# Reordering the scan step of a hybrid decoder kernel: where the held work, the spread and the meta rows stand

## The chip, the core and the metric

The kernel runs on one core of one Trainium2 chip. The metric is the device time of one execution in microseconds (us); the time given for a kernel is the median of its runs. A core has five engines that work through their own queues in order: TensorE (PE in the profile, with its weight loads shown apart as PEld), VectorE (DVE), ScalarE (ACT), GpSimd (POOL) and SyncE (SP, which here only issues DMAs).

## The reference

One decoder layer over 16 learned meta tokens and 512 tokens of width 1024, in float32. The part that matters here is the Mamba-2 branch: a projection, a causal convolution of four taps with SiLU, and a state-space scan in chunks of 128 positions, with the 16 meta tokens as a short chunk in front.

```python
u = rmsnorm(h, mix_norm_w)
proj = u @ w_in                      # pool | z | xbc | dt | gates
gates = sigmoid(proj[..., OFF_GATE:] + b_gate)
...
xbc = silu(causal_depthwise_conv(xbc, conv_w, conv_b))   # x (2048), B (8 x 128), C (8 x 128)
dt = softplus(dt_raw + dt_bias); a = -exp(a_log)
# per chunk, group g (8 of them) and head r (4 per group):
a_cs = cumsum(dt * a)
y_diag = einsum(C B^T, exp(a_cs_l - a_cs_s) masked, x * dt)
states = einsum(B, exp(a_cs_last - a_cs), x * dt)
# states are carried from chunk to chunk: prev = decay * prev + states
y_off = einsum(C, prev, exp(a_cs))
y = (y_diag + y_off + x * d_skip) * silu(z)
y = rmsnorm_per_group(y) * norm_w
...
h = h + (gate_pool * y_pool + gate_ssd * (y @ w_ssd_out)) @ w_o
h = h + square(relu(rmsnorm(h) @ w_ff1)) @ w_ff2
out = rmsnorm(h)[:, 16:]
```

## The kernel before

Every large product is made of three matmuls on parts: each float32 operand is split in a high part (a cast on ACT) and a low part (a subtraction on DVE), and high x high, low x high and high x low are summed in PSUM. Weights come in blocks of 128 x 1024 (`raw`, three buffers); `block()` hands out the next prepared block, and, with `depth` 2, first issues the DMA, the ACT cast `whi` (L75) and the DVE subtraction `wlo` (L76) of the block two places further on.

The work is staged: the first projections (group 0's tiles and three gates) on unnormalised input, then a loop over the eight SSD groups `g` (L640), then the pooling branch, the output projection, and the MLP. The change lies in the loop. In iteration `g` the kernel does the scan of group `g` and, in between, the projections of group `g+1`, so that PE has matmuls while ACT and DVE prepare the scan. The order on PE, ACT and DVE is the order of the program (`manual_schedule`); on each of these engines an instruction that waits holds up everything behind it.

The parts of one iteration, by the names of the code and the profile:

- `turn` (L416): PE turns B's three chunks and its meta rows (`ptb`), x's meta rows (`ptm`) and x's four chunks (`ptx`); ACT copies the meta rows to `bm` and the chunks to `btok`; DVE scales x's meta rows (`xdm`, then three parts `xm`), x's chunks by dt (`xdt`), by the decay (`xdd`), and forms the low part of `bm`.
- `steps`: the four projections for group `g+1`, in the order B (`bt`), C (`ct`), and the two tiles of x (`xc`), all called `px` on PE (L157 to L160; 48 matmuls each). Each returns its convolution: one ACT instruction (L347) and three on DVE (L350), all four of which read the projection's PSUM tile. In iteration 4 the steps are eight parts of the first half of the output projection (`pso`), and in iteration 7 eight parts of the second (`psp`); the first step of iteration 7 (`two`) does two parts.
- `spread` (L452): two exponentials into `eb`, which `gather` reads much later.
- `states` (L470): PE computes `pcb` (C by B) and `pst` (from `xdd` and `btok`, and one product from `xm` and `bm`, L485); ACT copies the first state; DVE carries the states on.
- `spans` and `decays`: per head four ACT instructions (L463), per pair of heads one exponential (L468), in place on `abc`.
- `scores` (L491, DVE, L493), `outputs` (L496, PE: `po`, then `py`), `gather`, `squares`, `norm`, `root`, `finish`: the sum of y, its norm, and the split rows `yh`, `yl` of the group's two tiles (L539 to L543).
- After the scan come z's projection (`pz`), and in iterations 1, 2, 3 and 6 a gate's projection (`pgp`).

What is left over at the end of an iteration is put into the list `held` and done by ACT and DVE in the next: the gate's sigmoid (L673) after iterations 1, 2, 3 and 6; z's SiLU (L666) after iterations 0, 4 and 5, and after 0 and 5 also `finish` of the second tile. `held` is emptied behind the first step and ahead of `spread`.

PSUM: the projections share two buffers of two banks (`psum2`), the small products of the scan four of one bank (`psum1`). So the third projection of an iteration (the first tile of x) needs the buffer of B's, and can begin when B's convolution has read it; the second needs the buffer of z's projection or the gate's, and can begin when z's SiLU or the sigmoid has read it.

Of the kernel before, what the change touches and what calls it, by code (L numbers as in the profile page):

```python
# [9 lines left out]
F32 = mybir.dt.float32  # L10
F32R = mybir.dt.float32r
AF = mybir.ActivationFunctionType
ALU = mybir.AluOpType

P = 128
D = 1024
SEQ = 512
NM = 16
# [4 lines left out]
R = 4  # L23
# [28 lines left out]
def kernel(ctx: ExitStack, tc, xT, x, w, vec, fnw, out):  # L52
    nc = tc.nc
    act, dve, pe, pool = nc.scalar, nc.vector, nc.tensor, nc.gpsimd
# [49 lines left out]
    ident = const.tile([P, P], F32, name="ident")  # L104
# [16 lines left out]
    def col(off, i, n=P):  # L121
        return vs[:n, off + i : off + i + 1]
# [5 lines left out]
    decm = const.tile([NM, HEADS], F32, name="decm")  # L128
# [10 lines left out]
    xm = gc.tile([MQ, R, HEAD], F32R, name="xm", bufs=1)  # L139
# [7 lines left out]
    def psum2(name):  # L147
        return psa.tile([P, 1024], F32, tag="mm", name=name)

    def psum1(name):  # L150
        return psb.tile([P, 512], F32, tag="s", name=name)
# [43 lines left out]
    b, raw, hi, lo = wdt  # L195
# [71 lines left out]
    for t, name in ((rsh, "dgh"), (rsl, "dgl")):  # L267
        d = pre.tile([NT, 6, NT], F32R, tag="sq", name=name, bufs=2)
# [3 lines left out]
    for i in range(2):  # L272
        pb = psum1(f"pb1_{i}")
        c = slice(3 * i, 3 * i + 3)
# [14 lines left out]
    for c in range(4):  # L289
        r = slice(c * H, (c + 1) * H)  # L290
# [20 lines left out]
    for c in (slice(0, P), slice(P, W)):  # L311
        n = c.stop - c.start
# [40 lines left out]
    def silu(t):  # L353
        act.activation(t, t, AF.Silu)

    def group_tiles(g):
        xc = gc.tile([P, 2, L], F32, tag="xc", name=f"xc{g}")
        bt = gc.tile([P, L], F32, tag="bt", name=f"bt{g}")
        ct = gc.tile([P, SEQ], F32, tag="ct", name=f"ct{g}")
        zt = gc.tile([P, 2, SEQ], F32, tag="zt", name=f"zt{g}", bufs=1)  # L360
        return xc, bt, ct, zt
# [28 lines left out]
    def xbc_tile(g, cur, n):  # L390
        dst, t, skip = tiles_of(g, cur)[n]
        runs, view = wide(psum2(f"px{g}_{t}"), skip)
        proj(runs, block(), U)
        return lambda: conv(dst, view, t)

    def z_half(ps, i, between=None):
        wblk = block()
        for k in range(NK):
            if k == 2 and between:
                between()  # L400
            proj_step(narrow(ps[:, i * SEQ : (i + 1) * SEQ]), k, wblk, U)


    def bc(ap, n):
        return ap.unsqueeze(len(ap.shape)).to_broadcast(list(ap.shape) + [n])

    class Scan:
# [8 lines left out]
        def turn(self):  # L416
            g, hs = self.g, self.hs
            xc, bt, ct, zt = self.cur
            self.xdt = xdt = gs.tile([P, 4, R, 64], F32, tag="xdt", name=f"xdt{g}")
            xdm = gs.tile([NM, R, 64], F32, tag="xdm", name=f"xdm{g}")  # L420
            self.btok = gs.tile([P, 3, P], F32, tag="btok", name=f"btok{g}")
            ptb = psum1(f"ptb{g}")
            for c in range(3):
                pe.transpose(ptb[:, c * P : (c + 1) * P], bt[:, tok(c)], ident)
            pe.transpose(ptb[:NM, 3 * P :], bt[:, :NM], ident)
            hi, mid, low = slice(0, NM), slice(32, 32 + NM), slice(64, 64 + NM)
            pbm = ptb[:NM, 3 * P :]
            act.copy(bm[hi], pbm)
            act.copy(bm[mid], pbm)
            act.copy(self.btok.rearrange("p c n -> p (c n)"), ptb[:, : 3 * P])  # L430
            pm = psum1(f"ptm{g}")
            for i in range(2):
                pe.transpose(pm[:NM, i * P : (i + 1) * P], xc[:, i, :NM], ident)
            dve.tensor_tensor(xdm, pm[:NM, :256].rearrange("p (r d) -> p r d", r=R),
                              bc(decm[:, hs], 64), op=ALU.mult)
            dve.tensor_copy(xm[hi], xdm)
            dve.tensor_copy(xm[low], xdm)
            dve.tensor_tensor(xm[mid], xdm, xm[hi].bitcast(F32), op=ALU.subtract)
            for b in range(2):
                pt = psum1(f"ptx{g}_{b}")  # L440
                for c in range(2):
                    for i in range(2):
                        o = c * 256 + i * P
                        pe.transpose(pt[:, o : o + P], xc[:, i, tok(2 * b + c)], ident)
                dve.tensor_tensor(xdt[:, 2 * b : 2 * b + 2, :, :],
                                  pt.rearrange("p (c r d) -> p c r d", c=2, r=R),
                                  bc(dtok[:, 0, 2 * b : 2 * b + 2, hs], 64), op=ALU.mult)
            self.xdd = gs.tile([P, 3, R, 64], F32, tag="xdd", name=f"xdd{g}")
            dve.tensor_tensor(self.xdd, xdt[:, :3, :, :], bc(dec[:, :3, hs], 64), op=ALU.mult)
            dve.tensor_tensor(bm[low], pbm, bm[hi].bitcast(F32), op=ALU.subtract)  # L450

        def spread(self):  # L452
# [98 lines left out]
    def gate_product(d, rhs=U):  # L551
        ps = psum2(f"pgp{d}")[:, :SEQ]
        proj(narrow(ps), block(), rhs)
        return ps
# [31 lines left out]
    def out_half(d):  # L586
        ps = psum2(f"pso{d}")[:, :SEQ]
        ssd_out(d, ps, range(8))
        return lambda: act.copy(acc[d], ps)
# [3 lines left out]
    def out_part(d):  # L593
        ps = psum2(f"psp{d}")[:, :SEQ]
        for k in range(8, 14):
            mm3(ps, next(part), ys[k], k == 8, k == 13)
        return lambda: dve.tensor_tensor(acc[d], acc[d], ps, op=ALU.add)

    held = []

    def scan_with(sc, steps):
        sc.turn()
        after = steps[0]()
        while held:
            held.pop(0)()
        sc.spread()
        after()
        sc.states()
        after = steps[1]()
        sc.spans((0, 1))  # L610
        sc.decays(0)
        sc.spans((2,))
        after()
        after = steps[2]()
        sc.spans((3,))
        sc.decays(1)
        sc.scores(0)
        sc.scores(1)
        after()
        sc.outputs()  # L620
        after = steps[3]()
        sc.gather(0)
        if len(steps) > 4:
            after()
            after = steps[4]()
        sc.gather(1)
        after()
        sc.squares()
        if len(steps) > 4:
            steps[5]()()  # L630
            sc.norm()
            after = steps[6]()
            sc.root()
            after()
            for step in steps[7:]:
                step()()
            sc.finish()

    with tc.manual_schedule(engines={mybir.EngineType.PE, mybir.EngineType.Activation, mybir.EngineType.DVE}):
        for g in range(G):  # L640
            sc = Scan(g, cur)
            if g + 1 == G:
                def two():
                    out_part(0)()
                    return out_part(1)

                scan_with(sc, [two] + [lambda d=d: out_part(d) for d in range(2, NK)])
                break
            nxt = group_tiles(g + 1)
            tiles = [lambda n=n: xbc_tile(g + 1, nxt, n) for n in range(4)]  # L650
            if g == 4:
                scan_with(sc, [lambda d=d: out_half(d) for d in range(NK)])
                for t in tiles:
                    t()()
            else:
                scan_with(sc, tiles)
            gate = GATE_AT.get(g)
            xc, bt, ct, zt = nxt
            ps = psum2(f"pz{g + 1}")
            z_half(ps, 0)  # L660
            for t in (bt, ct, xc.rearrange("p i t -> p (i t)")):
                silu(t)
            z_half(ps, 1, None if g == 4 else sc.norm)

            def z_silu(zt=zt, ps=ps):
                act.activation(zt.rearrange("p i t -> p (i t)"), ps, AF.Silu)  # L666

            if gate is not None:
                z_silu()
                pg = gate_product(gate)  # L670
                sc.root()
                sc.finish()
                held.append(lambda d=gate, pg=pg: act.activation(m1[d], pg, AF.Sigmoid, bias=col(V_BG, d)))  # L673
            else:
                held.append(z_silu)
                if g != 4:
                    sc.root()
                    sc.finish((0,))
                    held.append(lambda sc=sc: sc.finish((1,)))
            cur = nxt  # L680
    depth[0] = 0
    gc_stack.close()
# [160 lines left out]
    for n, d in enumerate(MERGE):  # L843
# [8 lines left out]
        for i, k in enumerate(ks):  # L852
            c = slice(k * P, (k + 1) * P)
# [100 lines left out]
    wo_prod(av, "S3", s3, False, False)  # L954
    pt = banks("ptA")
    turn(pt, 0, 0)
    onto(1, 1, alpha, SUB)
    turned(pt, 0, 0)
# [189 lines left out]
    c = NC - 1  # L1148
# [5 lines left out]
    for t in range(4):  # L1154
        T, st = t // 2, slice((t % 2) * P, (t % 2 + 1) * P)
        n = 0
        for half in range(2):
            parts = [(0, 512)] if half == 0 or t < 3 else [(0, 256), (256, 256)]
            for a, m in parts:
# [3 lines left out]
                i = 0  # L1163
                for k, seg in ((1, (A11, 3)[T]), (0, (A12, A22)[T])):
                    wh, wl = wq[k, half]
                    for p in range(2):
                        x0 = p * 512 + a
                        f = i == 0 and not (T == 0 and half == 0)
# [152 lines left out]
```

## Time and profile before

| | |
|---|---|
| median of 3 runs | 1025.28 us (1024.18 to 1026.62) |
| the profiled execution | 1026.65 us, of which 1023.7 us are the span of its instructions |
| PE busy | 98% of the span |
| DVE, ACT, POOL busy | 70%, 55%, 9% |
| DMA | 105.62 MB, 102 GB/s of HBM traffic over the span |
| mean granted TensorE clock | 0.996 |

Matmuls are pipelined and their ends are modelled: a matmul of 512 columns is listed with 0.39 us, and the next one begins 0.23 us after it. So a busy PE is read by the distances between starts and by its waits, not by the busy share alone. The iterations of the loop begin (first `ptb`) at 66.48, 108.76, 160.87, 209.51, 258.13, 344.93, 387.21 and 439.17 us.

### The profile page before, as it was taken

The numbers are of one execution on the slowest core, as the hardware profiler recorded it, in microseconds if no ns is written. First come the engines' busy times: TensorE is split into PE (matmuls) and PEld (weight loads), VectorE is DVE, ScalarE is ACT, GpSimd is POOL, SyncE is SP. The second block draws the span as 40 slices with busy tenths as digits, with TensorE's granted clock in tenths as the row PEclk, the third lists the DMA queues.
The fourth block names the chain that finished last, engine by engine and source line by source line (L and its number), as shares of the span: only waits on it lengthen the run. The fifth ranks groups of instructions, "written<-read, shape, count | busy, mean of one in ns | idle before, by whom it ended". The sixth has DMA issues, their size and how long they took to land.

```text
span 1023.7 us, 14027 instructions
## 1 busy us (share of the span) xinstructions
PE 1005.2 (98%) x5689; PEld 875.2 (85%) x5689; DVE 713.3 (70%) x894; ACT 561.3 (55%) x789; POOL 88.7 (9%) x52
## 2 busy tenths in 40 slices
PE   9999999999999999989999999999999999999997
PEld 8889899898889998878899888888888888888886
DVE  7978586867646585867855567975777567666866
ACT  7765858595843658575344333474545355454444
POOL 0100000000000000000000001003040421403400
PEclk9999999999999999999999999999999999999999
DMA  6243132323232231322622333224324323333112
GB/s 238 72 138 103 62 110 77 124 66 130 90 127 83 83 105 61 125 82 89 221 89 98 104 102 121 85 94 154 103 70 119 120 83 113 95 101 124 42 42 83
DMA packets 29281, 105.62 MB, mean 103 GB/s; under 512 B 3296, under 2 KB 4256, under 8 KB 28192
## 3 DMA queue, kind: packets, MB, share of 16 engines
q1 hardware_dynamic: 26496, 92.75, 27.1%
q0 software_dynamic: 2000, 11.08, 2.9%
q8 instruction: 44, 0.72, 0.3%
q10 hardware_dynamic: 720, 0.91, 0.3%
q14 instruction: 21, 0.17, 0.1%
HBM read 102.55 MB, written 2.16 MB: 102 GB/s over the span
## 4 chain that ended last, share of the span: by engine, by line
PE 84%; ACT 8%; DVE 6%; issue 1%; DMA 0%; SPq 0%; ACTq 0%
PE pf L100 6%; PE pf L99 6%; PE pf L101 6%; PE px L157 5%; PE px L158 4%; PE px L160 4%; PE alpha L1070 3%; PE alpha L1071 3%; PE alpha L1072 3%; PE pz L160 2%; PE pz L157 2%; PE pz L158 2%; PE py L509 2%; PE pp L160 1%; PE pp L158 1%; PE pp L157 1%
## 5 line engine op out<-in xcount | busy, mean ns | idle before, releaser
L76 DVE TENSOR_TENSOR wlo<-raw,whi 128x1024 fp32r<-128x1024 f32 (+1 forms) x131 | 163.9, 1253 | 112.8 <-ACT whi L75 112.6
L75 ACT CAST whi<-raw 128x1024 fp32r<-128x1024 f32 (+1 forms) x131 | 136.0, 1041 | 123.9 <-PE pf L100 55.8
L157 PE MATMUL px<-uh,whi 128*128 128x264 f32 (+1 forms) x448 | 120.1, 289 | 4.4 <-DVE bt L350 4.4
L158 PE MATMUL px<-ul,whi 128*128 128x264 f32 (+1 forms) x448 | 118.4, 285 | 0.0
L99 PE MATMUL pf<-vh,whi 128*128 128x512 f32 x256 | 99.9, 390 | 0.0
L101 PE MATMUL pf<-vh,wlo 128*128 128x512 f32 x256 | 99.8, 390 | 0.0
L100 PE MATMUL pf<-vl,whi 128*128 128x512 f32 x256 | 99.7, 390 | 0.0
L160 PE MATMUL px<-uh,wlo 128*128 128x264 f32 (+1 forms) x448 | 91.0, 285 | 0.0
L157 PEld LDWEIGHTS px<-uh,whi 128*128 128x128 f32 x448 | 85.7, 191 | 6.0 <-ACT abc L463 4.7
L158 PEld LDWEIGHTS px<-ul,whi 128*128 128x128 f32 x448 | 85.4, 191 | 0.0
L832 DVE TENSOR_TENSOR slo<-b,shi 128x1024 fp32r<-128x1024 f32 x35 | 49.1, 1404 | 31.6 <-ACT shi L831 31.6
L160 PEld LDWEIGHTS px<-uh,wlo 128*128 128x128 f32 x448 | 69.3, 189 | 0.0
L831 ACT CAST shi<-b 128x1024 fp32r<-128x1024 f32 x35 | 36.7, 1049 | 47.2 <-PE pf L100 36.4
L101 PEld LDWEIGHTS pf<-vh,wlo 128*128 128x128 f32 x256 | 48.1, 188 | 10.0
L99 PEld LDWEIGHTS pf<-vh,whi 128*128 128x128 f32 x256 | 48.1, 188 | 10.0
L100 PEld LDWEIGHTS pf<-vl,whi 128*128 128x128 f32 x256 | 48.1, 188 | 9.8
L1081 POOL TENSOR_TENSOR b<-b,b 128x1024 f32<-128x1024 f32 x14 | 35.6, 2546 | 238.3 <-DVE slo L832 238.3
L1070 PE MATMUL alpha<-shi,hh 128*128 128x512 f32 x140 | 54.7, 391 | 0.0
L1071 PE MATMUL alpha<-slo,hh 128*128 128x512 f32 x140 | 54.6, 390 | 0.0
L1072 PE MATMUL alpha<-shi,hl 128*128 128x512 f32 x140 | 54.6, 390 | 0.0
L897 DVE TENSOR_TENSOR ht<-ht,alpha 128x1024 f32<-128x1024 f32 x35 | 42.6, 1216 | 10.9 <-PE alpha L1072 10.9
L347 ACT ACTIVATE xc<-px,vs 128x528 f32<-128x528 f32 x14 | 11.1, 791 | 61.1 <-PE px L160 61.1
(418 smaller groups left out, 2515.4 us busy)
## 6 DMA issues: line engine op xcount, KB each, us to landing
raw<-in_w SPq DMA_DIRECT2D x129, 512.0 KB, 3.5
b<-in_w SPq DMA_DIRECT2D x28, 512.0 KB, 3.5
abc<-acs_d POOLq DMA_DIRECT2D x8, 1024.0 KB, 5.8
wob<-in_w SPq DMA_DIRECT2D x8, 512.0 KB, 5.3
xt<-in_xT SPq DMA_DIRECT2D x8, 264.0 KB, 5.2
ht<-in_x POOLq DMA_DIRECT2D x4, 512.0 KB, 6.1
w<-in_w SPq DMA_DIRECT2D x4, 512.0 KB, 3.5
out_dram<-out SPq DMA_DIRECT2D x4, 320.0 KB, 2.4
```

What stands on the lines that cost most here:

```text
L75: act.copy(hi[:, c], raw[:, c])
L76: dve.tensor_tensor(lo[:, c], raw[:, c], hi[:, c].bitcast(F32), op=ALU.subtract)
L99: pe.matmul(ps, ah, bh, start=first, stop=False)
L100: pe.matmul(ps, ah, bl, start=False, stop=False)
L101: pe.matmul(ps, al, bh, start=False, stop=last)
L157: pe.matmul(o, wh, rhs[0][k][:, c], start=k == 0, stop=False)
L158: pe.matmul(o, wh, rhs[1][k][:, c], start=False, stop=False)
L160: pe.matmul(o, wl, rhs[0][k][:, c], start=False, stop=k == NK - 1)
L832: dve.tensor_tensor(lo, src, hi.bitcast(F32), op=ALU.subtract)
L1070: pe.matmul(ps[t], a[0], wh[:, cs], start=f, stop=False, skip_group_check=True)
L1071: pe.matmul(ps[t], a[0], wl[:, cs], start=False, stop=False, skip_group_check=True)
L1072: pe.matmul(ps[t], a[1], wh[:, cs], start=False, stop=l, skip_group_check=True)
```

## The change

Three pieces, all in the loop; the instructions stay the same in kind and number.

- In `turn`, PE turns x's meta rows behind x's chunks, and DVE does `xdt` and `xdd` ahead of `xdm` and `xm`; ACT copies `btok` ahead of the two copies to `bm`.
- In `scan_with`, `held` (z's SiLU or the sigmoid) is emptied ahead of the first step, thus ahead of that step's weight cast; B's convolution comes next, and `spread` behind it; `finish` of the second tile moves to a list of its own, `rows`, behind `spread`.
- The spans of the third head move behind C's convolution and the third step's weight cast, to those of the fourth.

```diff
@@ turn
             pbm = ptb[:NM, 3 * P :]
+            act.copy(self.btok.rearrange("p c n -> p (c n)"), ptb[:, : 3 * P])
             act.copy(bm[hi], pbm)
             act.copy(bm[mid], pbm)
-            act.copy(self.btok.rearrange("p c n -> p (c n)"), ptb[:, : 3 * P])
-            pm = psum1(f"ptm{g}")
-            for i in range(2):
-                pe.transpose(pm[:NM, i * P : (i + 1) * P], xc[:, i, :NM], ident)
-            dve.tensor_tensor(xdm, pm[:NM, :256].rearrange("p (r d) -> p r d", r=R),
-                              bc(decm[:, hs], 64), op=ALU.mult)
-            dve.tensor_copy(xm[hi], xdm)
-            dve.tensor_copy(xm[low], xdm)
-            dve.tensor_tensor(xm[mid], xdm, xm[hi].bitcast(F32), op=ALU.subtract)
             for b in range(2):
                 pt = psum1(f"ptx{g}_{b}")
...
             dve.tensor_tensor(self.xdd, xdt[:, :3, :, :], bc(dec[:, :3, hs], 64), op=ALU.mult)
+            pm = psum1(f"ptm{g}")
+            for i in range(2):
+                pe.transpose(pm[:NM, i * P : (i + 1) * P], xc[:, i, :NM], ident)
+            dve.tensor_tensor(xdm, pm[:NM, :256].rearrange("p (r d) -> p r d", r=R),
+                              bc(decm[:, hs], 64), op=ALU.mult)
+            dve.tensor_copy(xm[hi], xdm)
+            dve.tensor_copy(xm[low], xdm)
+            dve.tensor_tensor(xm[mid], xdm, xm[hi].bitcast(F32), op=ALU.subtract)
             dve.tensor_tensor(bm[low], pbm, bm[hi].bitcast(F32), op=ALU.subtract)
@@ scan_with
-    held = []
+    held, rows = [], []
 
     def scan_with(sc, steps):
         sc.turn()
-        after = steps[0]()
         while held:
             held.pop(0)()
+        after = steps[0]()
+        after()
         sc.spread()
-        after()
+        while rows:
+            rows.pop().finish((1,))
         sc.states()
         after = steps[1]()
         sc.spans((0, 1))
         sc.decays(0)
-        sc.spans((2,))
         after()
         after = steps[2]()
-        sc.spans((3,))
+        sc.spans((2, 3))
         sc.decays(1)
@@ the loop
                     sc.finish((0,))
-                    held.append(lambda sc=sc: sc.finish((1,)))
+                    rows.append(sc)
```

## The prediction

> **What bounds the kernel now.** I read the page first, then PE's waits, then PE, ACT and DVE in order of time around each wait.
>
> ```profile
> span 1023.7 us, 14027 instructions
> PE 1005.2 (98%) x5689; PEld 875.2 (85%) x5689; DVE 713.3 (70%) x894; ACT 561.3 (55%) x789; POOL 88.7 (9%) x52
> ```
>
> PE is busy nearly all the time, and the change adds or removes no matmul. So the time can fall only by what PE waits, and rise only by new waits. The waits view for PE, inside the loop over the groups:
>
> ```profile
> PE px L157 <- DVE bt L350: 4.4, 2, 2.2
> PE psp L99 <- ACT m L673: 3.2, 1, 3.2
> PE pst L483 <- DVE xdd L449: 1.7, 5, 0.7
> PE py L509 <- ACT whi L75: 1.1, 1, 1.1
> ```
>
> These are 10.4 us in 9 waits, all with a releaser that the change moves. In order of time, PE around the waits of iteration 1:
>
> ```profile
> 116.10 1.05 PE L475 MATMUL pcb<-ct,bt 128*128 128x128 f32 x8
> 117.33 1.53 PE L483 MATMUL pst<-xdd,btok 128*128 128x256 f32 x6 [0.17 <-DVE xdd L449]
> 118.51 0.48 PE L485 MATMUL pst<-xm,bm 80*128 80x256 f32 x1
> 124.31 0.40 PE L160 MATMUL px<-uh,wlo 128*128 128x258 f32 x2
> 126.89 0.36 PE L157 MATMUL px<-uh,whi 128*128 128x264 f32 x1 [2.19 <-DVE bt L350]
> ```
>
> The second px (C's) would have been followed at 124.31 + 2 x 0.12 = 124.55, since these matmuls start 0.12 apart; the next came at 126.89. So the wait costs 2.34, and a listed idle time is about 0.15 short, because modelled ends overlap the next start. I add 0.15 per wait: 2.5 for the five on xdd, 4.7 for the two on bt, 3.35 for psp, 1.25 for py.
>
> Waits also cost clock. The windows view (columns: PE busy, PEld, DVE, ACT, POOL, granted clock, DMA):
>
> ```profile
> 124.99:128.40 3.41, 1.50 (x12) 1.54 (x13) 3.20 (x7) 3.38 (x10) 0.00 (x0) 1.00 0.00 0
> 128.40:131.81 3.41, 3.41 (x18) 3.41 (x17) 3.24 (x6) 3.41 (x8) 0.00 (x0) 0.50 0.02 5
> 401.47:404.88 3.41, 1.70 (x15) 1.49 (x13) 1.97 (x3) 3.38 (x8) 0.00 (x0) 1.00 0.00 0
> 445.84:449.25 3.41, 1.07 (x5) 0.90 (x6) 3.31 (x6) 3.36 (x4) 0.00 (x0) 1.00 0.00 0
> 449.25:452.67 3.42, 3.42 (x10) 2.68 (x9) 1.81 (x3) 2.29 (x3) 0.00 (x0) 0.50 0.58 158
> ```
>
> A stretch of 3.41 us in which PE was busy 1.50 or 1.07 is followed by one at half clock; 1.70 busy (the same wait in iteration 6) was not. Each halved stretch does half its work: 1.7 us lost, twice, 3.4 in all. The Trainium skill ("TensorE: Matmul & The Clock Gate", "Why this matters for your kernels") advises against PE-idle gaps over about 3 us, one idle window bringing the slow clock. Here a wait of 2.34 was enough; by the rule the first halved stretch would have another cause and stay, which is a rival below.
>
> **x's rows ahead of the meta rows (turn).** DVE in iteration 1:
>
> ```profile
> 113.39 0.41 DVE L434 TENSOR_TENSOR xdm<-ptm,decm 16x256 f32<-16x256 f32 x1
> 114.90 1.29 DVE L445 TENSOR_TENSOR xdt<-ptx,dtok 128x512 f32<-128x512 f32 x2
> 116.23 0.96 DVE L449 TENSOR_TENSOR xdd<-xdt,dec 128x768 f32<-128x768 f32 x1
> 117.22 0.28 DVE L450 TENSOR_TENSOR bm<-ptb,bm 16x128 fp32r<-16x128 f32 x1
> 118.67 0.75 DVE L539 SCALAR_TENSOR_TENSOR yt<-yt,vs,rs 128x512 f32<-128x512 f32 x1
> ```
>
> The meta rows' four instructions fill 113.39 to 114.90. With xdt first, xdd ends 1.51 earlier, at 115.68; the longest of the five waits was 0.7 + 0.15. All five go: **-2.5**. What is late next is L485, which needs xm and bm. These keep their end (117.50), 1.0 before L485 began; the largest vanished wait moves L485 up by 0.85, so it still just fits. PE's own reordering (two small transposes behind eight) costs nothing, since DVE is the later one, and btok ahead of bm moves two copies of 0.26. A restart after a wait is slower too:
>
> ```profile
> L483 PE MATMUL pst<-xdd,btok x48: 378/380/456, 74.7 to 456.0; 128*128 128x256 f32 x48
> ```
>
> The slowest took 0.08 more than the median; for seven waits that go, **-0.5**.
>
> **B's convolution ahead of the spread and the second rows (iterations 1 and 6).** ACT in iteration 1, with DVE's part behind it:
>
> ```profile
> 113.56 1.05 ACT L75 CAST whi<-raw 128x1024 fp32r<-128x1024 f32 x1
> 114.63 1.28 ACT L666 ACT_TABLE_LOAD   x1
> 115.92 1.03 ACT L666 ACTIVATE zt<-pz 128x1024 f32<-128x1024 f32 x1
> 119.45 0.62 ACT L542 CAST yh<-yt 128x512 fp32r<-128x512 f32 x1 [2.50 <-DVE yt L539]
> 121.39 2.14 ACT L457 ACTIVATE eb<-abc 64x1024 f32<-64x1024 f32 x2
> 123.55 0.79 ACT L347 ACTIVATE bt<-px,vs 128x528 f32<-128x528 f32 x1
> 125.44 2.45 ACT L463 ACTIVATE abc<-abc,dtok 128x128 f32<-128x128 f32 x8
> 127.93 1.06 ACT L468 ACTIVATE abc<-abc 128x1024 f32<-128x1024 f32 x1
> 132.98 1.06 ACT L468 ACTIVATE abc<-abc 128x1024 f32<-128x1024 f32 x1
> ...
> 124.38 2.37 DVE L350 SCALAR_TENSOR_TENSOR bt<-px,vs,bt 128x527 f32<-128x527 f32 x3 [3.58 <-ACT bt L347]
> 131.16 2.31 DVE L350 SCALAR_TENSOR_TENSOR ct<-px,vs,ct 128x512 f32<-128x512 f32 x3
> 133.39 1.22 DVE L76 TENSOR_TENSOR wlo<-raw,whi 128x1024 fp32r<-128x1024 f32 x1
> 134.52 2.35 DVE L493 TENSOR_TENSOR abc<-abc,cbm 128x1024 f32<-128x1024 f32 x2
> ```
>
> bt stands behind ACT's wait of 2.50 for the second rows and behind spread with a table load. In the new order ACT does from 113.56: table load 1.28, SiLU (1.0 to the next start), whi (1.0), bt from 116.9 (its matmuls on PE end about where pcb starts, 116.10), table load and exponentials to 121.0. DVE: wlo 117.5 to 118.65, bt's three to 121.05 instead of 126.75. C's px ends at 124.2 by then (124.55 less pst's 0.35), so the wait on bt is gone with 3 us to spare: 2 x 2.35 = **-4.7**, and the halved stretch of iteration 1 with it, **-1.7**.
>
> What is late next is py, which needs the scores. Second rows: yt 121.0 to 121.75, yh to 122.4, state copy and whi to 123.6 (1.2, as 124.25 to 125.44). So the spans begin 1.85 earlier than 125.44. The third head's spans (1.2) are now behind C's convolution: its ACT part follows the first decays at 127.05 (127.93 - 1.85 + 0.97), DVE's part runs 127.8 to 130.1 (2.23 to wlo, as 131.16 to 133.39), wlo to 131.2, first scores to 132.4, second to 133.55; the second decays end at 134.04 - 1.85 = 132.2, in time. PE: x's px from 124.2 takes 5.9 (C's took 124.55 - 118.82 = 5.73, for 258 columns where this has 264), po 1.9 (16 of 0.12), so py is reached at 132.0 and waits for 132.4 + 0.1, then once more about 0.2 for the second scores: 0.65. Iteration 1 had no such wait (its px2 was late): **+0.65**. Iteration 6 has the same order and pays 0.65 where it paid 1.25: **-0.6**.
>
> **The sigmoid ahead of the first step (iterations 2, 3, 4, 7).** Only iteration 7 waits for it.
>
> ```profile
> 439.82 1.04 PE L444 MATMUL ptx<-ident,xc 128*128 128x128 f32 x8
> 444.13 1.99 ACT L75 CAST whi<-raw 128x1024 fp32r<-128x1024 f32 x2
> 446.14 1.28 ACT L673 ACT_TABLE_LOAD   x1
> 447.44 0.69 ACT L673 ACTIVATE m<-pgp,vs 128x512 f32<-128x512 f32 x1
> ```
>
> Two casts move behind it: 2.0 earlier, so psp waits 1.35 instead of 3.35: **-2.0**. A wait of 1.35 leaves at least 2.06 busy in any stretch of 3.41, more than the 1.70 that kept its clock: **-1.7**. The casts come 2.0 later, for blocks two places ahead, which PE reaches after the psp of 4.1 us (18 matmuls of 0.23) it is in. SP's and POOL's queues issue what they did, in the same order.
>
> **Sum:** -2.5 - 0.5 - 4.7 - 1.7 + 0.65 - 0.6 - 2.0 - 1.7 = -13.05. The profiled execution took 1026.65 (2.95 around its span), 1.37 over the median; taken from the median, 1025.28 - 13.0 = **1012.3**. Bounds: py's waits between none (-1.3) and twice that (+1.3), sums of small waits too short for the view (-0.9): 1010.0 to 1014.0.
>
> **Rivals.**
> 1. *The halved stretches stay* (the rule of the page named above, for one of them; or the grid of 3.41 falls badly on psp's 1.35): +1.7 to +3.4, 1014.0 to 1015.7. Against it: both came right behind the two emptiest windows. 0.06.
> 2. *The scores' chain takes over.* bt now stands ahead of the spread, and ACT waits for px at it. In iterations 0 and 5 the exponentials used to fill that wait:
>
> ```profile
> 74.02 0.79 ACT L347 ACTIVATE bt<-px,vs 128x528 f32<-128x528 f32 x1 [0.88 <-PE px L160]
> ```
>
> There table load and exponentials (3.4) slip behind bt, of which the old wait for the states (from 74.7 to 76.3) takes 1.6: up to 1.9 later scores, twice, and 0.65 doubled in 1 and 6: +5, 1017.3. For it: iteration 6 waits for this chain already. Against: in 0 and 5 py shows no wait. 0.09.
> 3. *pcb gets the PSUM buffer of ptb* by the new order of allocation and waits for the last bm (117.50) instead of starting at 116.1: 1.4 in iterations 1, 2, 3, 4, 6: +7, 1019.3. 0.04.
> 4. *Slower: the first px takes the wrong buffer.* With held emptied first, both psum2 buffers have a reader ahead in the program when the first step asks for one. If it gets the one of pz or pgp, PE stands from ptx's end (439.82 + 0.87 in iteration 7) to the sigmoid (446.1): 5.4, in six iterations (4 has it too), about 33 with halved clocks still to come: 1012.3 + 33 = 1045. It decides from 2.2 each. Against: psp waits for the sigmoid (m L673) though the program had already freed another buffer by the add of the first psp; buffers seem to go by when they come free, and then the last x tile's is first. 0.08.
> 5. *Nothing:* each wait passes to another releaser of the same length, 1024 to 1026. Against: DVE's bt ends 3 us ahead of need. 0.03.
>
> **How the numbers follow.** Forecast 0.70, rivals 0.06, 0.09, 0.04, 0.08, 0.03. The range 1009.8 to 1016.0 holds the forecast with its bounds, the first rival and a small part of the second. Less than 0.2% (2 us) can't be told from no change here. Faster: 0.70 + 0.06 + 0.09 + 0.04 = 0.89; same 0.03; slower 0.08.
>
> **What would show it.** Right: in PE's waits px on bt and pst on xdd are gone, psp on the sigmoid near 1.2, py about 0.5 in iterations 1 and 6, clock 1.00 throughout the loop. Wrong: a first px or pcb with a wait, py waits in every iteration, or a stretch at 0.50 inside the loop.

## The result, and the profile after

The changed kernel takes 1012.68 us (median of 4 runs, 1012.34 to 1012.97) against 1025.95 us for the kernel before in the same runs (1024.18 to 1026.98): 13.3 us less, a ratio of 0.9872 with a 95% interval of 0.9855 to 0.9889. The profiled execution took 1012.34.

```profile
span 1010.5 us, 14027 instructions
PE 999.8 (99%) x5689; PEld 871.5 (86%) x5689; DVE 712.3 (70%) x894; ACT 560.6 (55%) x789; POOL 88.7 (9%) x52
```

The instructions are as many as before. PE's listed busy time is 5.4 us shorter, mostly because no matmul of the loop runs at half clock any more (two stretches of 3.41 us, each of which did half its work). The waits of PE, largest first:

```profile
PE py L509 <- ACT abc L468: 1.5, 2, 0.8
PE pdt L201 <- DVE ones_r L109: 1.5, 1, 1.5
PE psp L99 <- ACT m L674: 1.2, 1, 1.2
PE pt_dt L319 <- DVE ddt L308: 0.3, 1, 0.3
```

Of the four waits of the kernel before that the change was aimed at, px on bt and pst on xdd are gone, psp's fell from 3.2 to 1.2 and py's grew from 1.1 in one iteration to 1.5 in two; the other two rows belong to the first stage. (L674 is the sigmoid, L667 z's SiLU, L436 and L437 are `ptx` and `xdt` in the changed kernel.)

A shorter ruler than the span shows that nothing else moved. Two PE rows mark the loop, the first turn and the first projection of the pooling branch; before, then after:

```profile
66.48 0.49 PE L424 MATMUL ptb<-ident,bt 128*128 128x128 f32 x3
485.22 0.28 PE L157 MATMUL pp<-uh,whi 128*128 128x264 f32 x1
```

```profile
66.13 0.49 PE L424 MATMUL ptb<-ident,bt 128*128 128x128 f32 x3
471.96 0.28 PE L157 MATMUL pp<-uh,whi 128*128 128x264 f32 x1
```

From the one to the other it was 418.74 us and is 405.83, 12.91 less. The first stage differs by 0.35, which it does between executions of any of these kernels (the first turn stands between 66.1 and 67.6 in all of them), and from the pooling projection to the end it was 538.5 both times. This stretch is called the loop time below. By iteration, from one first `ptb` to the next (the last one up to the pooling projection):

| iteration | 0 | 1 | 2 | 3 | 4 | 5 | 6 | 7 |
|---|---|---|---|---|---|---|---|---|
| before | 42.28 | 52.11 | 48.65 | 48.62 | 86.80 | 42.28 | 51.96 | 46.05 |
| after | 42.28 | 48.75 | 47.72 | 47.72 | 85.87 | 42.28 | 48.78 | 42.44 |
| gain | 0 | 3.36 | 0.93 | 0.90 | 0.93 | 0 | 3.18 | 3.61 |

Iteration 1 in order of time, ACT and DVE, with the same instructions as in the prediction:

```profile
113.57 1.28 ACT L667 ACT_TABLE_LOAD   x1
114.87 1.03 ACT L667 ACTIVATE zt<-pz 128x1024 f32<-128x1024 f32 x1
115.79 1.03 ACT L75 CAST whi<-raw 128x1024 fp32r<-128x1024 f32 x1
116.72 0.80 ACT L347 ACTIVATE bt<-px,vs 128x528 f32<-128x528 f32 x1
118.83 2.14 ACT L457 ACTIVATE eb<-abc 64x1024 f32<-64x1024 f32 x2
121.62 0.62 ACT L542 CAST yh<-yt 128x512 fp32r<-128x512 f32 x1 [0.65 <-DVE yt L539]
123.36 2.45 ACT L463 ACTIVATE abc<-abc,dtok 128x128 f32<-128x128 f32 x8
130.89 1.06 ACT L468 ACTIVATE abc<-abc 128x1024 f32<-128x1024 f32 x1
...
114.72 0.96 DVE L441 TENSOR_TENSOR xdd<-xdt,dec 128x768 f32<-128x768 f32 x1
117.11 0.28 DVE L450 TENSOR_TENSOR bm<-ptb,bm 16x128 fp32r<-16x128 f32 x1
118.57 2.36 DVE L350 SCALAR_TENSOR_TENSOR bt<-px,vs,bt 128x527 f32<-128x527 f32 x3
129.84 1.22 DVE L76 TENSOR_TENSOR wlo<-raw,whi 128x1024 fp32r<-128x1024 f32 x1
130.97 2.35 DVE L493 TENSOR_TENSOR abc<-abc,cbm 128x1024 f32<-128x1024 f32 x2
```

ACT no longer stands 2.50 us for the second rows; the wait is 0.65 and comes behind bt. bt's last DVE instruction ends at 120.93, where it ended at 126.75 (5.5 earlier when counted from the iteration's start, which is itself 0.35 earlier), and PE comes to the first x projection some 3 us later. PE at what is late next:

```profile
129.60 1.95 PE L503 MATMUL po<-ct,st 128*128 128x128 f32 x16
132.29 2.18 PE L509 MATMUL py<-abc,xdt 128*64 128x128 f32 x32 [0.75 <-ACT abc L468]
```

py begins when the first scores have ended (130.97 + 1.22 = 132.19 and a tenth), though the view names the last decays. In the iterations where py doesn't wait it begins 1.87 behind `po` (87.32 and 89.19 in iteration 0), and the next px 1.90 behind that; so here it could have begun at 131.47. The wait is 0.82, and 0.21 is lost once more inside py, at the second scores (134.41 is 2.11 behind 132.29). Together these are 1.03, which is what iteration 1 is longer than 2 and 3; in iteration 6 they are 1.05.

### The profile page after: what moved, and what is told of

It is laid out like the page before. It is cut to its first block, busy times and chain, and to the rows that moved or that the text cites. A ratio compares the mean times of both kernels' runs of the same rounds, so it can differ in the third digit from the quotient of the medians.

```text
span 1010.5 us, 14027 instructions
## 1 busy us (share of the span) xinstructions
PE 999.8 (99%) x5689; PEld 871.5 (86%) x5689; DVE 712.3 (70%) x894; ACT 560.6 (55%) x789; POOL 88.7 (9%) x52
## 4 chain that ended last, share of the span: by engine, by line
PE 84%; DVE 7%; ACT 7%; issue 1%; DMA 0%; SPq 0%; DVEq 0%; ACTq 0%
PE pf L99 6%; PE pf L100 6%; PE pf L101 6%; PE px L157 3%; PE px L158 3%; PE px L160 3%; PE alpha L1071 3%; PE alpha L1072 3%; PE alpha L1073 3%; PE pz L160 2%; PE pz L157 2%; PE pz L158 2%; PE pp L157 2%; PE pp L160 2%; PE pp L158 2%; PE pso L99 1%
## 5 line engine op out<-in xcount | busy, mean ns | idle before, releaser
L157 PE MATMUL pz<-uh,whi 128*128 128x512 f32 x112 | 43.7, 390 | 0.0
```

The source lines that it names most:

```text
L157: pe.matmul(o, wh, rhs[0][k][:, c], start=k == 0, stop=False)
```

## The experiments

The theory was that each wait of PE ends when a chain on ACT and DVE is done, so that time is gained only where that chain itself ends earlier and no later wait takes the gain back. The rivals were additive waits, and the slower rival of the prediction. Loop times come from the same two rows as above, the time from the medians of the runs made together (ratio with its 95% interval).

| kernel | time, us | before, same runs | ratio | loop, us | against |
|---|---|---|---|---|---|
| turn alone | 1024.31 | 1025.33 | 0.9990 (0.9980 to 0.9999) | 417.82 | before: -0.92 |
| all but turn | 1015.09 | 1025.33 | 0.9898 (0.9883 to 0.9913) | 408.24 | before: -10.50 |
| held first alone | 1021.63 | 1025.33 | 0.9963 (0.9949 to 0.9977) | 414.74 | before: -4.00 |
| convolution first alone | 1039.74 | 1025.33 | 1.0140 (1.0125 to 1.0155) | 432.80 | before: +14.06 |
| spans back | 1019.38 | 1025.95 | 0.9940 (0.9925 to 0.9956) | 414.79 | after: +8.96 |
| rows held | 1017.95 | 1025.95 | 0.9924 (0.9910 to 0.9939) | 411.22 | after: +5.39 |
| late cast | 1012.12 | 1025.95 | 0.9869 (0.9854 to 0.9883) | 405.21 | after: -0.62 |
| late cast, sigmoid in the gap | 1011.16 | 1025.95 | 0.9857 (0.9841 to 0.9873) | 404.30 | after: -1.53 |
| the same, late norm | 1010.53 | 1025.78 | 0.9856 (0.9836 to 0.9876) | 403.80 | after: -2.03 |
| the changed kernel again | 1012.43 | 1025.78 | 0.9877 (0.9859 to 0.9895) | 405.78 | after: -0.05 |

**Turn alone, and all but turn.** The kernel before with the new `turn`, and the changed kernel with the old one.

> The kernel before with the new order in turn alone. Shifted waits (my theory: a wait of PE ends when the chain on ACT and DVE is done, so a wait that is removed ahead of it on PE only makes the later one longer): the five waits on xdd go, but in iterations 1 and 6 the wait on bt grows from 2.35 to about 2.8, in 2 and 3 the wait at py grows from 0.25 to about 0.75, and only iteration 4 keeps its gain: about 1.0 us faster than before. Additive waits (the sum in the prediction): 3.0 us faster.

> The changed kernel with the old order in turn: all of the change but the transposes and meta rows. Shifted waits: the waits on xdd come back in iterations 1, 2, 3, 4 and 6, but in 1 and 6 py's wait is shorter by as much, so only 2, 3 and 4 pay, 0.6 + 0.6 + 0.95: about 2.1 us over the changed kernel, 1014.8, 11 faster than before. Additive waits: 3.0 over the changed kernel, 1015.7. With the run of turn alone: if the waits add, the two parts' gains sum to 13; if they shift, to about 12.

Measured: 0.92 and 10.50 off the loop, together 11.42 where the whole change takes off 12.91. The turn is worth 0.92 by itself and 2.41 on top of the rest. PE's waits with the turn alone say why:

```profile
PE px L157 <- DVE bt L350: 4.9, 2, 2.5
PE psp L99 <- ACT m L673: 3.2, 1, 3.2
...
PE py L509 <- ACT whi L75: 1.3, 2, 0.6
```

The row for xdd is gone, and with it 2.5 us of waits; px's row has grown from 4.4 to 4.9, and py, which waited 1.1 in iteration 6, now waits 0.6 in 2 and in 3. bt and the scores ended when they had ended before, and PE only came to them earlier. The longer wait in iteration 6 also emptied its stretch enough for a halved one behind it, which the kernel before did not have. Shifted waits, not additive ones. With all but the turn, the waits on xdd are back (0.69 in iterations 1 and 6, 0.50, 0.49 and 0.86 in 2, 3 and 4), and py's in 1 and 6, ahead of its first matmul, fell from 0.82 to 0.17.

**Held first, and convolution first, each alone.**

```diff
         sc.turn()
-        after = steps[0]()
         while held:
             held.pop(0)()
+        after = steps[0]()
         sc.spread()
```

> The kernel before with one move alone: what is held (sigmoid or z's SiLU, and the second rows) ahead of the first step. Theory: psp's wait on the sigmoid falls from 3.35 to 1.35 and the halved stretch behind it goes, -3.7; the waits on bt stay near 2.2 with the halved stretch of iteration 1; the first px waits for nothing: 1022. Rival (the slower one of the prediction): the first px gets the buffer of z's or the gate's projection and waits some 5 us in six iterations: over 1050.

Measured: -4.00 in the loop. The first px waits for nothing, so the slower rival's buffer does not come about; psp waits 1.46, its halved stretch is gone, and the one of iteration 1 has stayed:

```profile
PE px L157 <- DVE bt L350: 4.0, 2, 2.0
PE pst L483 <- DVE xdd L449: 1.7, 5, 0.7
...
PE psp L99 <- ACT m L673: 1.3, 1, 1.3
PE py L509 <- ACT whi L75: 1.1, 1, 1.1
```

```diff
         after = steps[0]()
+        after()
         while held:
             held.pop(0)()
         sc.spread()
-        after()
```

> The kernel before with one move alone: B's convolution right behind the first step, ahead of what is held and of the spread. Theory: the SiLU or sigmoid now stands behind ACT's wait for the first px, and the second px, which needs the buffer that the SiLU or sigmoid frees, waits about 2.3 in iterations 1, 2, 3 and 6 and 1 in 5, the states' product up to 1 in 1 and 6, and py some 2.5 in 1 and 6; psp in iteration 7 stays: about 10 us slower than before, 1035, and more where a stretch is halved. Rival (each move is worth the wait it is aimed at): the two waits on bt and a halved stretch go, 6 us faster, 1019.

Measured: 14.06 slower, where 10 were expected, and the wait on bt is gone. So the move to which the prediction gives the largest gain is a loss by itself. (By itself it also puts B's convolution ahead of the SiLU or sigmoid, which the whole change doesn't.) But the waits are others than expected: the second px waits only 0.3 to 0.4 per iteration, and py takes the most. Four stretches are halved, where it was two.

```profile
PE py L509 <- ACT xc L347: 12.7, 5, 4.6
PE psp L99 <- ACT m L673: 3.2, 1, 3.2
PE pst L483 <- DVE xdd L449: 2.4, 5, 0.7
```

ACT in iteration 1 of this kernel:

```profile
117.47 0.79 ACT L347 ACTIVATE bt<-px,vs 128x528 f32<-128x528 f32 x1 [1.33 <-PE px L160]
118.28 1.28 ACT L666 ACT_TABLE_LOAD   x1
119.58 1.02 ACT L666 ACTIVATE zt<-pz 128x1024 f32<-128x1024 f32 x1
123.26 0.62 ACT L542 CAST yh<-yt 128x512 fp32r<-128x512 f32 x1 [2.66 <-DVE yt L539]
125.20 2.14 ACT L457 ACTIVATE eb<-abc 64x1024 f32<-64x1024 f32 x2
128.71 2.45 ACT L463 ACTIVATE abc<-abc,dtok 128x128 f32<-128x128 f32 x8
```

ACT now waits 1.33 at bt with the SiLU still to do, and then 2.66 for the second rows; the spans begin at 128.71 instead of 125.44, the first scores, which stand behind them, end at 138.71 instead of 135.74, and py, which needs these, waits 4.65. In the whole change ACT does SiLU or sigmoid in the time of that wait, and the rows come behind the spread.

**The other two pieces undone.** The changed kernel with the third head's spans ahead of C's convolution again, and the changed kernel with the second rows in `held` (`held.append(lambda sc=sc: sc.finish((1,)))`).

> The changed kernel with the third head's spans back ahead of C's convolution. Theory (scores' chain ends PE's wait at py): C's convolution, the third cast and so the first scores come 1.2 later, py's waits in iterations 1 and 6 grow from 0.9 to over 2, small ones come in 2 and 3: 4 to 5 us over the changed kernel, 1017. Rival: no wait of the kernel before named the spans, so their place is worth nothing: 1012.7.

> The changed kernel with the second rows back in what is held, now ahead of the first step and of B's convolution. Theory: ACT waits for DVE's yt ahead of the first cast and bt, everything behind it on ACT and DVE comes about 1.5 later in iterations 1 and 6; bt has 3 us to spare, the scores have not: no wait on bt, py's waits there grow to about 2.5: 3.4 us over the changed kernel, 1016. Rival: the rows have to be behind bt for bt's sake, and the wait on bt comes back with 2.3 twice and a halved stretch: 1018 and a wait on bt in the view.

Measured: +8.96 and +5.39 in the loop. Neither has a wait on bt; both pay at py, with the spans

```profile
PE py L509 <- ACT xc L347: 4.4, 2, 2.2
...
PE py L509 <- issue: 0.7, 2, 0.4
```

and with the rows held

```profile
PE py L509 <- ACT abc L468: 5.3, 2, 2.7
```

Both rivals fall: the spans have a price though no wait of the kernel before named them, and the rows' place matters for the scores, not for bt. The size was short because the py waits of over 2 us empty their stretch: both of them with the spans back, one with the rows held.

```profile
132.88:136.29 3.41, 1.21 (x19) 0.98 (x20) 3.41 (x4) 2.32 (x3) 0.00 (x0) 1.00 0.40 96
136.29:139.70 3.41, 3.41 (x23) 3.08 (x24) 3.34 (x5) 0.00 (x0) 0.53 (x1) 0.50 0.16 60
```

With the spans back, the loop without the two halved stretches (3.4) is still 5.5 longer where 4 to 5 were expected: py waits 0.21 and loses as much again inside in iterations 0 and 5 too, and in 1 and 6 x's meta rows wait for the logarithm of the group before.

```profile
PE ptm L444 <- ACT rs L533: 0.6, 2, 0.3
```

The profiled execution was the longest of four, and the median is only 6.7 over the changed kernel. The other three have no trace, but their granted clocks are on record: 1018.28 and 1018.69 at 0.999, 1020.06 at 0.997, the profiled 1021.55 at 0.995. A halved stretch takes 0.0017 off the mean clock, so these read as executions with none, none, one and two of them, and the two without are 5.6 and 6.0 over the changed kernel, much as the loop without its halved stretches is. With the rows held, py's two waits are 2.75 where they were 0.82, 3.8 more together, and with the one halved stretch (1.7) that makes about the 5.4.

**Beyond the change.** The waits left in the changed kernel are py's and psp's. The late cast takes the third step's weight block out of the way of the scores:

```diff
+        late = len(steps) == 4
+        if late:
+            depth[0] = 1
         after = steps[2]()
         sc.spans((2, 3))
         sc.decays(1)
         sc.scores(0)
         sc.scores(1)
+        if late:
+            depth[0] = 2
+            prepare(2)
```

> The changed kernel with the block that the third step prepares (cast on ACT, subtraction on DVE) moved behind the second scores, in the iterations with four steps. Theory: both scores come 0.95 to 1.15 earlier, py's two waits of about 1.08 in iterations 1 and 6 go: 2.0 us faster than the changed kernel, 1010.6. Rival: the wait is for the state products or for the last decays alone, or z's projection now waits for its late block: no change, or slower.

Measured: only 0.62 less in the loop. py's two waits of 1.03 and 1.05 are gone as expected, but not a third of that was gained, since the next chain came due: the norm's second matmul, which stands behind two of the eight parts of z's second half, now waits for DVE in iterations 1 and 6, 0.50 each, and 0.75 with the slower starts around it (48.47 against 47.72 in the iterations without a wait).

```profile
PE psp L99 <- ACT m L680: 1.2, 1, 1.2
...
PE png L529 <- DVE qlg L250: 0.4, 2, 0.2
```

The sigmoid between the two tiles' rows, and the norm later:

```diff
-                sc.finish()
-                held.append(lambda d=gate, pg=pg: act.activation(m1[d], pg, AF.Sigmoid, bias=col(V_BG, d)))
+                sc.finish((0,))
+                act.activation(m1[gate], pg, AF.Sigmoid, bias=col(V_BG, gate))
+                sc.finish((1,))
```

and for the late norm besides

```diff
-    def z_half(ps, i, between=None):
+    def z_half(ps, i, between=None, at=2):
...
-            if k == 2 and between:
+            if k == at and between:
...
-            z_half(ps, 1, None if g == 4 else sc.norm)
+            z_half(ps, 1, None if g == 4 else sc.norm, 2 if gate is None else 5)
```

> As the one with the late cast, and the gate's sigmoid between the two tiles' finishing at the end of the iteration, in the 1.4 us for which ACT there waits for DVE, instead of held into the next. Theory: the sigmoid ends some 2.8 earlier in iteration 7, psp's wait of 1.37 goes; the second tile's rows come 0.55 later, and the first psp, which reads them, waits for at most 0.4: 1.0 to 1.4 faster than with the late cast, 1009.4. Rival: the rows' delay passes to psp and to the turn in full: same as with the late cast.

> As the one with the late cast and the sigmoid in the gap, and in the iterations with a gate the norm's two matmuls stand behind five of the eight parts of z's second half instead of behind two. Theory: with py's wait gone, DVE's chain to the norm was next, 0.50 in iterations 1 and 6; the norm's rows are then in time, ACT has to wait for z there anyway, and the loop takes 1.0 less than with the sigmoid in the gap, 403.3, and about 2.5 less than in the changed kernel: 1010.1. Rival: the logarithm, the rows and the turn come later by as much, and the wait goes on to the turn of the next iteration: no change.

> The changed kernel once more, in the same runs: 1012.7, and 405.8 from the first turn to the first pooling projection.

Measured: 0.91 less with the sigmoid in the gap (psp's row is gone), and 0.50 less again with the late norm, half of what was expected. Iterations 1 and 6 fell by 0.73 and 0.75, while 2 and 7 rose by 0.41 and 0.54: the rows and the turn behind the norm come later, and the states' last product (L485, 0.3 in iteration 2) and the first psp now wait for them. Both the theory and its rival hold in part. This kernel is the fastest of all, 1010.53 (1010.19 to 1010.98) beside 1012.43 (1012.05 to 1013.98) for the changed kernel in the same runs. PE's largest wait that is left in its loop:

```profile
PE psp L100 <- DVE yl L543: 0.2, 1, 0.2
```

## Why the prediction was right, point by point

The forecast was 13.0 us less; the medians say 13.3, the loop of the profiled executions 12.91. That they agree so closely is in part luck: the executions of the kernel before lie between 1023.5 and 1027.0, and those with the highest granted clock on record (four at 0.997) are the shortest, 1023.5 to 1023.8.

- *PE's waits are all there is to gain.* Held: the iterations without a listed wait, 0 and 5, took 42.28 before and after.
- *x's rows ahead of the meta rows, 3.0.* xdd ends at 115.68, the figure worked out (though 0.35 later than that when counted from the loop's start), and all five waits went; the longest matmul of `pst` fell from 456 to 382 ns, so the restarts went too. Iterations 2, 3 and 4, which had little else, gained 0.93, 0.90 and 0.93. But the term stands only beside the others: turn alone was worth 0.92. The sum treated it as separate, and got away with it because the rest of the change made the later waits short; the py waits of 2 and 3, which went as well (by the starts in the kernel before 0.15 ahead of py and 0.21 inside it, in each), were left out of the sum.
- *B's convolution first, 4.7 and a halved stretch.* bt ends 5.8 earlier by the clock of the profile (5.7 worked out) and 5.5 earlier from the iteration's start, 3 us ahead of need. By the rule of the Trainium skill that the prediction weighed ("TensorE: Matmul & The Clock Gate", "Why this matters for your kernels") the halved stretch of iteration 1 would have stayed. It went with the wait of 2.34, so here the measurement decides against the rule: a gap of 3 us is not needed.
- *py next, 0.65 in iterations 1 and 6.* This is the term that was mis-sized: 0.82 and 0.21, so 1.03, and 1.05 in iteration 6, which paid 1.39 before (1.18 and 0.21) and so gained 0.34 instead of 0.6. The first scores ended at 132.19 against 132.4; PE could have begun py at 131.47 against 132.0. Both are to be read with the loop's start 0.35 earlier here, so the scores were 0.1 late and PE 0.2 early. On PE's side the x projection began 0.07 earlier than worked out and took 5.82 instead of 5.9, `po` 1.87 instead of 1.9. On the side of the scores, ACT and DVE came to iteration 1 late, which belongs to the second rival below.
- *The sigmoid, 2.0 and a halved stretch.* psp waited 1.37 against 1.35, and the stretch around it was 2.20 us busy and kept its clock:

```profile
434.72:438.13 3.41, 2.20 (x10) 1.52 (x9) 3.25 (x8) 3.40 (x4) 0.00 (x0) 1.00 0.00 0
```

- *The rivals.* The second showed half of its face. In iteration 0 ACT indeed waits for px at bt, and everything behind comes later:

```profile
73.67 0.79 ACT L347 ACTIVATE bt<-px,vs 128x528 f32<-128x528 f32 x1 [4.04 <-PE px L160]
77.95 0.37 ACT L486 COPY st<-pst 128x256 f32<-128x256 f32 x1
98.53 1.06 ACT L522 ACTIVATE sqg<-yt 128x1024 f32<-128x1024 f32 x1 [0.52 <-DVE yt L518]
```

The state copy is 1.6 later than the 76.3 of before and the spans 1.7, near the price of up to 1.9. The first scores, with the third head's spans now behind C's convolution, are only 0.6 later (86.92 against 86.34; 0.9 from the loop's start) and end 1.0 before PE comes to py, so there is no wait in iterations 0 and 5. But the delay goes on: ACT now waits 0.52 for `yt` at the squares, where it waited for nothing before, and ACT and DVE come to the turn of iteration 1 no earlier than in the kernel before (`yh` at 112.14 and 112.13), though PE does by 0.35. That is a part of py's wait in 1 and 6, which this rival put at 1.3 and the forecast at 0.65. No run takes it away by itself. The slower rival's buffer did not appear in any run, whether `held` was emptied first or not; the other rivals left no trace.

That the sum came out was helped by two errors of opposite sign: py was put 0.38 too low in iteration 1 and its gain in iteration 6 0.26 too high, 0.6 together, and the waits at py in iterations 2 and 3, 0.7 together, were left out. A forecast of a part by itself would have failed by more: additive working gives 3.0 for the turn (0.92 measured) and 6 us of gain for the convolution first (14 of loss).

## What to carry to other kernels

Where PE's waits decide the time of a loop, a wait ends with a chain on other engines, and it is worth what that chain's end moves, less what the next chain takes back; work out each edit against the next wait, not against its own. An order of work has to be judged whole: one piece of this change, put alone into the kernel before, costs more than the whole change gains. When a wait is removed, look at the stretch of 3.4 us around it, since a half-empty one costs as much again in clock.

## What the runs showed of the hardware

The clock was halved for a stretch of 3.41 us, on a fixed grid, behind each stretch at full clock in which PE's listed busy time was 1.5 us or less (twelve in the loops of the kernels run here, 0.43 to 1.5), and behind none at full clock with 1.59 or more. The two nearest to the bound are the 1.50 of the kernel before, quoted in the prediction, and the first of these, with the convolution first alone, which was followed by a stretch at full clock:

```profile
132.65:136.06 3.41, 1.59 (x15) 1.40 (x13) 1.87 (x3) 3.41 (x9) 0.00 (x0) 1.00 0.45 154
136.06:139.47 3.41, 0.66 (x12) 0.69 (x14) 3.41 (x4) 2.81 (x4) 0.00 (x0) 1.00 0.21 67
139.47:142.88 3.41, 3.41 (x28) 2.98 (x25) 3.34 (x5) 0.00 (x0) 0.53 (x1) 0.50 0.22 87
```

So an idle share of a little over half of a stretch is enough, and a wait of some 2 us costs 1.7 more or not, by where it falls. Once halved, more seems to be asked for, though only one case shows it: in the same kernel a halved stretch with 2.74 us busy, behind psp's wait, was followed by a second halved one, while a halved stretch that was busy throughout was always the last.

```profile
460.32:463.74 3.42, 2.74 (x7) 2.17 (x8) 3.36 (x5) 3.37 (x4) 0.00 (x0) 0.50 0.17 50
463.74:467.15 3.41, 3.41 (x10) 2.65 (x9) 0.15 (x1) 0.66 (x1) 0.00 (x0) 0.50 0.77 234
```
